# Softmax denominators of a second attention layer carried across partitions by way of DRAM in place of TensorE transposes

## The chip, the cores and the metric

The kernel runs on one core of a Trainium2 chip. The core has five engines that run side by side, each with its own queue of instructions: TensorE (PE, matrix products and transposes, with weight loads shown apart as PEld), VectorE (DVE), ScalarE (ACT), GpSimd (POOL) and SyncE (SP, which here only issues DMA transfers). SBUF and PSUM have 128 partitions. The metric is the device time of one execution in microseconds (us); lower is better. The times quoted are of whole executions, and a profile is one further execution with the hardware profiler on.

## What is computed

The reference is a trunk of two layers over 1024 positions of width 1024. The first layer is a dilated window attention in three groups; it is not touched here. The second is multi-head latent attention with 16 heads, each of 64 value columns, and it ends in a gate, an output product and a layer norm. The part that matters:

```python
def block(args):
    qn, qr = args
    s = (jnp.einsum('bqhd,bkhd->bhqk', qn, k_nope)
         + jnp.einsum('bqhd,bkd->bhqk', qr, k_rope)).astype(jnp.float32) * scale
    p = jax.nn.softmax(s, axis=-1).astype(v.dtype)
    return jnp.einsum('bhqk,bkhd->bqhd', p, v)
...
y = o * jax.nn.silu(gate)
return y @ w_out
```

The kernel does not normalise `p`. It takes exp(s - max) and its row sum, multiplies the unnormalised weights with the values, and puts the reciprocal of the row sum (the "denominator" below) into the product with the gate.

## The kernel before

The layout decides everything about the denominators. The scores of one unit `u` (head `hd = u // 8`, 128 queries `t = u % 8`) lie as queries on partitions by 1024 keys on columns, so a row sum is one number per partition. The output of weights times values (`po`) and the gate `gT` lie the other way: 64 value columns on 64 partitions, queries along the columns. So each denominator, one number on a query's partition, has to reach 64 partitions at that query's column.

The loop of `layer_b_attention` goes over 128 units, with the parts of several units interleaved:

- `front(u)`: six matmuls of 128x512 make the scores `s` (three products of split high and low parts, for two halves of the keys).
- `soft(u)`: DVE takes the row maximum, negated (L1251).
- `middle(u - 2)`: PE transposes the eight 128x128 pieces of the exponentials (L1270), ACT copies the rounded high part `pth` (L1273), DVE makes the low part `ptl` (L1274). Then DVE takes the reciprocal of the row sum (L1275), and POOL spreads it over 64 columns of a tile `den` of 128x128, one half for each unit of a pair (L1276).
- `expo(u)`: ACT takes the exponential with its row sum beside it (L1257).
- `back(w)`, once per pair of units: PE transposes `den` into columns 256 to 383 of the PSUM bank `po` (L1285), then makes 16 matmuls of weights times values into columns 0 to 255 (L1293). ACT copies the two halves of the product to SBUF (L1298, L1299). DVE multiplies the transposed denominators with the gate, in two pieces of 64x128 (L1302). POOL adds the two halves (L1305) and multiplies the sum with what DVE made, back into `gT` (L1306).

Beside the units the loop carries the preparation of the next pair of heads, step by step, in generators advanced at fixed places: `b_weights(p + 1)` loads the weights of the next pair of heads (L1109, and for every second pair L1117) and splits them into high and low parts on ACT (L1110) and POOL (L1111); `b_turn` and `b_qk` multiply with them on PE (`m` in the profile). For odd `p` the call of `b_weights(p + 1)` stands at `r = u % 16 = 1`, and the first product of `b_turn(p + 1)` follows on PE at the end of `r = 2`; for even `p` the first product with the new weights is that of `b_qk` from `r = 8` on. In the last pair of heads the loop loads the output weights (`b_wo_load`, L1353) instead. After the loop, `layer_b_out` loads rows of the norm and the gate (L781, L776) and the residual (L1395), and finishes the rows 128 at a time.

What sets the order: this part of the program stands in `tc.manual_schedule(engines=FIXED)` with `FIXED = {PE, SP}`. PE and SP run their instructions in the order in which the code writes them. The order of ACT, DVE and POOL is worked out when the program is built, from a simulated timeline. Each engine then runs its own queue strictly in order, so an instruction that waits holds all that stand behind it on its engine; SP's queue is where all loads of this layer are issued.

Two pools matter for the change: `M` (single tiles with tags) and `DR` (tiles in DRAM). `normb` and `ktab` in `layer_b_in` are two constant tables, used by `latents` (L983 to L1010) before the attention begins.

Of the kernel before, what the change touches and what calls it, by code (L numbers as in the profile page):

```python
# [15 lines left out]
F32 = mybir.dt.float32  # L16
F32R = mybir.dt.float32r
AF = mybir.ActivationFunctionType
ALU = mybir.AluOpType
# [4 lines left out]
P = 128  # L24
# [17 lines left out]
def f32(ap):  # L42
    return ap.bitcast(F32)
# [23 lines left out]
class Trunk:  # L67
# [877 lines left out]
    def layer_b_in(self):  # L945

        nc, A = self.nc, self.A
        wl = self.wl
        nb = self.M.tile([P, 384], F32, name="normb")
        nc.sync.dma_start(nb, A["bnorm"].to_broadcast([P, 384]))  # L950
        nc.vector.tensor_scalar(nb[:, 0:256], nb[:, 0:256], 96.0**-0.5, None, op0=ALU.mult)
        ktab = self.M.tile([P, 8, 2, 16], F32, name="ktab")
        nc.sync.dma_start(ktab, A["ktab"])
        U = [[(self.gt(F32R, "u1h"), self.gt(F32R, "u1l")) for _ in range(2)] for _ in range(4)]
        self.lat = [(self.gt(F32R, "lath"), self.gt(F32R, "latl")) for _ in range(3)]
# [275 lines left out]

    def layer_b_attention(self):
        nc = self.nc
        st = {}

        def front(u):
            hd, t = u // 8, u % 8
# [15 lines left out]

        def expo(u):
            s, m = st[u]
            pr = self.ht(F32, "pr")
            nc.scalar.activation(pr, s, AF.Exp, bias=m[:, 0:1], accum_out=m[:, 1:2])  # L1257
            st[u] = (pr, m)

        def middle(u):  # L1260
            pr, m = st.pop(u)
            a = u % 2
            if a == 0:
                st["pt"] = [(self.gt(F32R, "pth"), self.gt(F32R, "ptl")) for _ in range(2)]
                st["den"] = self.M.tile([P, P], F32, tag="den", bufs=3, name=self.nm("den"))
            for j in range(2):
                pt = self.PB.tile([P, 512], F32, tag="t", bufs=4, name=self.nm("t"))
                for c in range(4):
                    kt = 4 * j + c
                    nc.tensor.transpose(pt[:, c * P : c * P + P], pr[:, kt * P : kt * P + P], self.ident)  # L1270
                h, l = (x.rearrange("p (k q) -> p k q", k=4)[:, :, a * P : a * P + P] for x in st["pt"][j])
                src = pt.rearrange("p (k q) -> p k q", k=4)
                nc.scalar.copy(h, src)  # L1273
                nc.vector.tensor_tensor(l, src, f32(h), op=ALU.subtract)  # L1274
            nc.vector.reciprocal(m[:, 2:3], m[:, 1:2])  # L1275
            nc.gpsimd.tensor_copy(st["den"][:, 64 * a : 64 * a + 64], m[:, 2:3].to_broadcast([P, 64]))  # L1276
            if a:
                st[("pv", u // 2)] = (st.pop("pt"), st.pop("den"))

        def back(w):  # L1280
            pts, den = st.pop(("pv", w))
            hd, t0 = w // 4, (w % 4) * 256
            e = hd % 2
            po = self.PB.tile([P, 512], F32, tag="t", bufs=4, name=self.nm("o"))
            nc.tensor.transpose(po[:, 256:384], den, self.ident)  # L1285
            hq = hd % 4
            n = 0
            for j in range(2):
                for c in range(4):
                    kt = 4 * j + c  # L1290
                    v = self.vq[kt // 2][:, (kt % 2) * 512 + hq * P : (kt % 2) * 512 + hq * P + P]
                    for x in range(2):
                        nc.tensor.matmul(po[:, 0:256], v, pts[j][x][:, c * 256 : c * 256 + 256], start=n == 0, stop=n == 15)  # L1293
                        n += 1
            mine, other = slice(64 * e, 64 * e + 64), slice(64 - 64 * e, 128 - 64 * e)
            g = self.gT[hd // 2][mine, t0 : t0 + 256]
            w3 = self.ht(F32, "osum")
            nc.scalar.copy(w3[mine, 0:256], po[other, 0:256])  # L1298
            nc.scalar.copy(w3[mine, 512:768], po[mine, 0:256])  # L1299
            for a in range(2):  # L1300
                qs = slice(a * P, a * P + P)
                nc.vector.tensor_tensor(  # L1302
                    w3[mine, 256 + a * P : 384 + a * P], po[64 * a : 64 * a + 64, 256:384], g[:, qs], op=ALU.mult
                )
            nc.gpsimd.tensor_tensor(w3[mine, 0:256], w3[mine, 512:768], w3[mine, 0:256], op=ALU.add)  # L1305
            nc.gpsimd.tensor_tensor(g, w3[mine, 0:256], w3[mine, 256:512], op=ALU.mult)  # L1306

        nu = 128
        prep, vprep = iter(()), self.b_v(0)
# [1 line left out]
        for u in range(nu + 4):  # L1311
            p, r = u // 16, u % 16
# [22 lines left out]
            if 0 <= u - 2 < nu:  # L1335
                middle(u - 2)
                next(vprep, None)
            if u < nu:
                expo(u)
            if u == nu:  # L1340
                self.b_out_blocks(0, range(4))
            if u == nu + 1:
                self.b_out_blocks(1, range(4))
            if u >= 4 and u % 2 == 0 and u < nu + 4:
                back((u - 4) // 2)
# [194 lines left out]
```

## Time and profile before

| what | value |
|---|---|
| time of the kernel, median of 3 runs | 1395.11 us (1394.83 to 1395.6) |
| the profiled execution, whole | 1399.57 us |
| its span from first to last instruction | 1397.8 us |
| mean granted TensorE clock over the span | 0.993 |
| second attention, first to last unit (from the timeline) | about 811 to 1304 us |
| output part behind it | about 1304 to 1398 us |

The profiled execution is a little longer than the median of the timed runs, so sums made in its numbers are carried to the median as differences. In the profile a line such as `L1285 PE MATMUL o<-ident,den x64: 270/273/302` names the kernel line, the engine, the operation, the tile written and the tiles read, the count, and the least, median and largest duration in ns. Matmuls are pipelined, and the next one begins before the one before it ends, so what one costs is read from the distance between starts, which the chain of work shows. `SPq` stands for DMA issues on SP's queue. "Waits" say which engine stood still until which other one had finished.

### The profile page before, as it was taken

How to read it: one execution, taken by the hardware profiler on the slowest of the kernel's cores; microseconds unless marked ns; L12 is line 12 of the kernel's file. 1: busy time of each engine (PE TensorE's matmuls, PEld its weight loads, DVE VectorE, ACT ScalarE, POOL GpSimd, SP SyncE). 2: the span in 40 equal slices, each digit the busy share in tenths (PEclk: the TensorE clock that was granted, in tenths of full speed). 3: DMA queues.
4: the chain of work that ended last, by engine and by line, in shares of the span. 5: the costliest groups of instructions: out<-in, count | busy, mean ns of one | idle time of the engine just before them, and what ended most of it. 6: DMA issues, size and time to landing. Idle time of an engine off the chain costs nothing.

```text
span 1397.8 us, 21019 instructions
## 1 busy us (share of the span) xinstructions
PE 1355.3 (97%) x7523; PEld 1160.8 (83%) x7523; DVE 938.9 (67%) x1708; ACT 820.3 (59%) x1604; POOL 573.6 (41%) x657
## 2 busy tenths in 40 slices
PE   6999999999999999999999999999999999999897
PEld 5788888888888788888987888888889888898786
DVE  7654354555455492746745178898988889888787
ACT  3575565565443452425752178788787878888321
POOL 5341233132122226903742254634463463444653
PEclk9999999999999999999999999999999999999999
DMA  9422211022244302544145001010010100014132
GB/s 356 112 64 36 59 50 50 25 60 73 95 151 123 99 31 77 180 149 151 61 119 166 21 14 37 16 30 16 22 29 18 35 16 16 16 61 133 49 113 83
DMA packets 39721, 105.26 MB, mean 75 GB/s; under 512 B 5126, under 2 KB 11270, under 8 KB 39617
## 3 DMA queue, kind: packets, MB, share of 16 engines
q1 hardware_dynamic: 35608, 91.80, 21.3%
q0 software_dynamic: 3552, 12.06, 3.5%
q8 instruction: 60, 0.98, 0.3%
q14 instruction: 45, 0.36, 0.1%
q10 hardware_dynamic: 456, 0.05, 0.0%
HBM read 87.60 MB, written 8.43 MB: 69 GB/s over the span
## 4 chain that ended last, share of the span: by engine, by line
PE 74%; DVE 12%; ACT 5%; issue 4%; DMA 4%; SPq 0%; POOL 0%; DVEq 0%; ACTq 0%
PE pj L89 7%; PE pj L91 7%; PE pj L90 7%; PE o L1293 5%; PE t L1270 5%; PE po L89 4%; PE po L91 4%; PE po L90 4%; DVE mb L1251 3%; PE s L91 3%; PE s L89 3%; PE s L90 3%; PE pg L89 2%; PE pg L90 2%; PE pg L91 2%
## 5 line engine op out<-in xcount | busy, mean ns | idle before, releaser
L89 PE MATMUL pj<-uh,wh 128*128 128x512 f32 x528 | 216.0, 409 | 0.0
L91 PE MATMUL pj<-uh,wl 128*128 128x512 f32 x528 | 207.4, 393 | 0.0
L90 PE MATMUL pj<-ul,wh 128*128 128x512 f32 x528 | 207.4, 393 | 0.0
L1274 DVE TENSOR_TENSOR ptl<-t,pth 128x512 fp32r<-128x512 f32 x256 | 165.4, 682 | 3.0 <-ACT pth L1273 0.9
L1251 DVE TENSOR_REDUCE mb<-s 128x1 f32<-128x1024 f32 x128 | 155.8, 1217 | 7.9 <-PE s L91 6.3
L1257 ACT ACTIVATE pr<-s,mb 128x1024 f32<-128x1024 f32 x128 | 143.4, 1120 | 29.2 <-DVE mb L1251 21.1
L1273 ACT CAST pth<-t 128x512 fp32r<-128x512 f32 x256 | 138.9, 589 | 36.2 <-PE t L1270 34.1
L102 POOL TENSOR_TENSOR wl<-wraw,wh 128x1024 fp32r<-128x1024 f32 x43 | 106.6, 2485 | 106.7 <-ACT wh L101 54.6
L1270 PEld LDWEIGHTS t<-ident,pr 128*128 128x128 f32 x1024 | 119.3, 140 | 19.7 <-DVE ptl L1274 2.6
L1270 PE MATMUL t<-ident,pr 128*128 128x128 f32 x1024 | 133.2, 272 | 1.9 <-DVE ptl L1274 1.9
L1293 PE MATMUL o<-pth,vq 128*128 128x256 f32 x512 | 130.4, 292 | 0.0
L1293 PE MATMUL o<-ptl,vq 128*128 128x256 f32 x512 | 125.5, 283 | 0.8 <-DVE ptl L1274 0.8
L507 ACT ACTIVATE sb<-sb,stat 128x256 f32<-128x256 f32 (+1 forms) x144 | 67.0, 467 | 98.6 <-DVE stat L501 98.5
L91 PEld LDWEIGHTS pj<-uh,wl 128*128 128x128 f32 x528 | 99.4, 188 | 22.2
L1276 POOL COPY den<-mb 128x64 f32<-128x64 f32 x128 | 30.1, 236 | 203.2 <-DVE mb L1275 193.6
L90 PEld LDWEIGHTS pj<-ul,wh 128*128 128x128 f32 x528 | 100.1, 190 | 14.3
L89 PEld LDWEIGHTS pj<-uh,wh 128*128 128x128 f32 x528 | 99.9, 189 | 14.5
L89 PE MATMUL s<-kb,q 128*128 128x512 f32 x256 | 104.4, 408 | 0.2 <-ACT pr L1257 0.2
L91 PE MATMUL s<-kb,q 128*128 128x512 f32 x256 | 101.3, 396 | 0.0
L90 PE MATMUL s<-kb,q 128*128 128x512 f32 x256 | 100.8, 394 | 0.0
L1293 PEld LDWEIGHTS o<-ptl,vq 128*128 128x128 f32 x512 | 97.7, 191 | 1.4 <-DVE ptl L1274 1.4
L1293 PEld LDWEIGHTS o<-pth,vq 128*128 128x128 f32 x512 | 97.7, 191 | 0.2
(288 smaller groups left out, 3317.6 us busy)
## 6 DMA issues: line engine op xcount, KB each, us to landing
wraw<-wa SPq DMA_DIRECT2D x36, 512.0 KB, 4.9
ada<-ada_row SPq DMA_DIRECT2D x64, 256.0 KB, 3.6
wraw<-wo_a SPq DMA_DIRECT2D x18, 512.0 KB, 3.6
ada<-ada_ss SPq DMA_DIRECT2D x16, 512.0 KB, 8.2
kb<-kb POOLq DMA_DIRECT2D x30, 256.0 KB, 3.4
xc<-xt SPq DMA_DIRECT2D x8, 512.0 KB, 9.2
xr<-x SPq DMA_DIRECT2D x8, 512.0 KB, 5.7
xn_d<-z POOLq DMA_DIRECT2D x8, 512.0 KB, 4.6
```

Of the source, the lines that this page charges most:

```text
L89: mm(out, wh, xh, start=start, stop=False)
L90: mm(out, wh, xl, start=False, stop=False)
L91: mm(out, wl, xh, start=False, stop=stop)
L102: (lo_engine or self.nc.gpsimd).tensor_tensor(l[:, :width], raw[:, :width], f32(h[:, :width]), op=ALU.subtract)
L507: nc.scalar.activation(sb[:, a * w : a * w + w], sb[:, a * w : a * w + w], AF.Exp, bias=stat[:, 0, hh, t : t + 1], scale=-1.0, accum_out=s ...
L1251: nc.vector.tensor_reduce(m[:, 0:1], s, axis=AX.X, op=ALU.max, negate=True)
L1257: nc.scalar.activation(pr, s, AF.Exp, bias=m[:, 0:1], accum_out=m[:, 1:2])
L1270: nc.tensor.transpose(pt[:, c * P : c * P + P], pr[:, kt * P : kt * P + P], self.ident)
L1273: nc.scalar.copy(h, src)
L1274: nc.vector.tensor_tensor(l, src, f32(h), op=ALU.subtract)
L1276: nc.gpsimd.tensor_copy(st["den"][:, 64 * a : 64 * a + 64], m[:, 2:3].to_broadcast([P, 64]))
L1293: nc.tensor.matmul(po[:, 0:256], v, pts[j][x][:, c * 256 : c * 256 + 256], start=n == 0, stop=n == 15)
```

## The change

The denominators of a head are kept together in one tile `dens[hd]` of 128x8, one column per unit, written by the exponential itself. After every fourth unit, so once per 512 queries of a head (32 times in all), `spread` takes the reciprocal of four columns in one DVE instruction, stores them to a DRAM tile `den_d` so that the 512 numbers lie in the order of the queries (128 partitions with 4 numbers each, every number a separate run of 4 bytes in DRAM), and loads them back as one row of 512 numbers repeated on the 64 partitions of this head's half. Both transfers are issued on SP. The spreading on POOL (L1276), the transposes on PE (L1285) and the products on DVE (L1302) go. In `back` POOL multiplies the sum of the halves with the gate directly, and after every second pair it multiplies 64x512 of `gT` with the loaded denominators. The two tables of `layer_b_in` now use the buffers of the new tile `rden`.

```diff
--- before.py
+++ after.py
@@ -946,10 +946,11 @@
 
         nc, A = self.nc, self.A
         wl = self.wl
-        nb = self.M.tile([P, 384], F32, name="normb")
+        nb = self.M.tile([P, 512], F32, tag="rden", bufs=2, name="normb")[:, 0:384]
         nc.sync.dma_start(nb, A["bnorm"].to_broadcast([P, 384]))
         nc.vector.tensor_scalar(nb[:, 0:256], nb[:, 0:256], 96.0**-0.5, None, op0=ALU.mult)
-        ktab = self.M.tile([P, 8, 2, 16], F32, name="ktab")
+        ktab = self.M.tile([P, 512], F32, tag="rden", bufs=2, name="ktab")
+        ktab = ktab[:, 0:256].rearrange("p (i a c) -> p i a c", i=8, a=2)
         nc.sync.dma_start(ktab, A["ktab"])
         U = [[(self.gt(F32R, "u1h"), self.gt(F32R, "u1l")) for _ in range(2)] for _ in range(4)]
         self.lat = [(self.gt(F32R, "lath"), self.gt(F32R, "latl")) for _ in range(3)]
@@ -1231,7 +1232,8 @@
 
     def layer_b_attention(self):
         nc = self.nc
-        st = {}
+        st, dens, rden = {}, {}, {}
+        den_d = self.DR.tile([16, 1024], F32, name="den_d")
 
         def front(u):
             hd, t = u // 8, u % 8
@@ -1253,16 +1255,29 @@
 
         def expo(u):
             s, m = st[u]
+            hd, t = u // 8, u % 8
+            if t == 0:
+                dens[hd] = self.M.tile([P, 8], F32, tag="den", bufs=3, name=self.nm("den"))
             pr = self.ht(F32, "pr")
-            nc.scalar.activation(pr, s, AF.Exp, bias=m[:, 0:1], accum_out=m[:, 1:2])
-            st[u] = (pr, m)
+            nc.scalar.activation(pr, s, AF.Exp, bias=m[:, 0:1], accum_out=dens[hd][:, t : t + 1])
+            st[u] = pr
+
+        def spread(hd, z):
+
+
+            d = dens[hd][:, 4 * z : 4 * z + 4]
+            nc.vector.reciprocal(d, d)
+            ld = den_d[hd]
+            nc.sync.dma_start(bass.AP(ld.tensor, ld.offset + 512 * z, [[1, P], [P, 4]]), d)
+            t = rden[hd, z] = self.M.tile([P, 512], F32, tag="rden", bufs=2, name=self.nm("rden"))
+            mine = slice(64 * (hd % 2), 64 * (hd % 2) + 64)
+            nc.sync.dma_start(t[mine, :], den_d[hd : hd + 1, 512 * z : 512 * z + 512].to_broadcast([64, 512]))
 
         def middle(u):
-            pr, m = st.pop(u)
+            pr = st.pop(u)
             a = u % 2
             if a == 0:
                 st["pt"] = [(self.gt(F32R, "pth"), self.gt(F32R, "ptl")) for _ in range(2)]
-                st["den"] = self.M.tile([P, P], F32, tag="den", bufs=3, name=self.nm("den"))
             for j in range(2):
                 pt = self.PB.tile([P, 512], F32, tag="t", bufs=4, name=self.nm("t"))
                 for c in range(4):
@@ -1272,17 +1287,14 @@
                 src = pt.rearrange("p (k q) -> p k q", k=4)
                 nc.scalar.copy(h, src)
                 nc.vector.tensor_tensor(l, src, f32(h), op=ALU.subtract)
-            nc.vector.reciprocal(m[:, 2:3], m[:, 1:2])
-            nc.gpsimd.tensor_copy(st["den"][:, 64 * a : 64 * a + 64], m[:, 2:3].to_broadcast([P, 64]))
             if a:
-                st[("pv", u // 2)] = (st.pop("pt"), st.pop("den"))
+                st[("pv", u // 2)] = st.pop("pt")
 
         def back(w):
-            pts, den = st.pop(("pv", w))
+            pts = st.pop(("pv", w))
             hd, t0 = w // 4, (w % 4) * 256
             e = hd % 2
             po = self.PB.tile([P, 512], F32, tag="t", bufs=4, name=self.nm("o"))
-            nc.tensor.transpose(po[:, 256:384], den, self.ident)
             hq = hd % 4
             n = 0
             for j in range(2):
@@ -1296,14 +1308,13 @@
             g = self.gT[hd // 2][mine, t0 : t0 + 256]
             w3 = self.ht(F32, "osum")
             nc.scalar.copy(w3[mine, 0:256], po[other, 0:256])
-            nc.scalar.copy(w3[mine, 512:768], po[mine, 0:256])
-            for a in range(2):
-                qs = slice(a * P, a * P + P)
-                nc.vector.tensor_tensor(
-                    w3[mine, 256 + a * P : 384 + a * P], po[64 * a : 64 * a + 64, 256:384], g[:, qs], op=ALU.mult
-                )
-            nc.gpsimd.tensor_tensor(w3[mine, 0:256], w3[mine, 512:768], w3[mine, 0:256], op=ALU.add)
-            nc.gpsimd.tensor_tensor(g, w3[mine, 0:256], w3[mine, 256:512], op=ALU.mult)
+            nc.scalar.copy(w3[mine, 256:512], po[mine, 0:256])
+            nc.gpsimd.tensor_tensor(w3[mine, 0:256], w3[mine, 256:512], w3[mine, 0:256], op=ALU.add)
+            nc.gpsimd.tensor_tensor(g, w3[mine, 0:256], g, op=ALU.mult)
+            if w % 2:
+                z = (w % 4) // 2
+                g = self.gT[hd // 2][mine, z * 512 : z * 512 + 512]
+                nc.gpsimd.tensor_tensor(g, g, rden.pop((hd, z))[mine, :], op=ALU.mult)
 
         nu = 128
         prep, vprep = iter(()), self.b_v(0)
@@ -1337,6 +1348,8 @@
                 next(vprep, None)
             if u < nu:
                 expo(u)
+                if u % 4 == 3:
+                    spread(u // 8, (u % 8) // 4)
             if u == nu:
                 self.b_out_blocks(0, range(4))
             if u == nu + 1:
```

## The prediction

> **What bounds the kernel now.** I read the page's busy shares first, then the chain that ended last, then the stage that the change touches, cut into the 61 us that one pair of heads takes.
>
> ```profile
> PE 1355.3 (97%) x7523; PEld 1160.8 (83%) x7523; DVE 938.9 (67%) x1708; ACT 820.3 (59%) x1604; POOL 573.6 (41%) x657
> PE 74%; DVE 12%; ACT 5%; issue 4%; DMA 4%; SPq 0%; POOL 0%; DVEq 0%; ACTq 0%
> ```
>
> PE is busy for nearly the whole span and holds most of the chain. An average says little of one stage, so the next view is the table by stretches (columns: PE, PEld, DVE, ACT, POOL busy us, clock, DMA share, GB/s).
>
> ```profile
> 872.00:933.00 61.00, 59.71 (x385) 52.30 (x384) 54.96 (x96) 47.42 (x92) 33.72 (x49) 1.00 0.09 21
> 1177.00:1238.00 61.00, 60.70 (x411) 54.67 (x410) 53.54 (x94) 50.66 (x99) 21.62 (x39) 1.00 0.12 30
> sum 493.00, PE 487.36 PEld 432.49 DVE 429.67 ACT 399.91 POOL 227.90; mean PE 60.92 PEld 54.06 DVE 53.71 ACT 49.99 POOL 28.49
> ```
>
> In the second attention (the sum is over 811 to 1304 us) PE is busy 487.4 of 493 us, DVE 429.7, ACT 399.9 and POOL 227.9. PE is the bound, with DVE close behind. What PE waits for there is in the view of waits of PE (total us, times, longest):
>
> ```profile
> PE m L89 <- DVE kb L1222: 2.4, 7, 0.4
> PE t L1270 <- DVE ptl L1274: 1.9, 3, 0.6
> PE o L1293 <- DVE ptl L1274: 0.8, 3, 0.3
> PE s L89 <- ACT pr L1257: 0.2, 1, 0.2
> PE o L1285 <- DVE ptl L1274: 0.2, 1, 0.2
> ```
>
> They add up to 5.5 us, 5.3 of them on DVE. So in this stage a PE instruction taken away is worth its pitch, and work taken off DVE is worth at most these 5.3 us.
>
> **The change part by part.** First, what PE loses. The chain of waits in a stretch without preparation shows PE back to back:
>
> ```profile
> 1243.52 0.87 PE t L1270 x8
> 1244.39 0.11 PE o L1285
> 1244.50 1.91 PE o L1293 x16
> ...
> 1250.08 0.87 PE t L1270 x8
> 1250.95 0.11 PE o L1285
> 1251.06 1.91 PE o L1293 x16
> ```
>
> A pair of units takes 1250.08 - 1243.52 = 6.56 us, and the transpose of `den` is 0.11 us of it, once per pair. 64 pairs x 0.11 = **7.0 us** less on PE, all on the path.
>
> Second, what DVE and POOL lose and gain (groups by line: busy us, mean ns).
>
> ```profile
> L1302 DVE TENSOR_TENSOR osum<-o,gT 64x128 f32<-64x128 f32 x128 | 36.8, 288 | 35.5 <-ACT osum L1299 31.6 <-PE s L90 1.2 <-POOL den L1276 0.6
> L1276 POOL COPY den<-mb 128x64 f32<-128x64 f32 x128 | 30.1, 236 | 203.2 <-DVE mb L1275 193.6 <-PE t L1270 6.9 <-PE o L1293 2.4
> L1203 POOL TENSOR_TENSOR q<-rope,q 64x512 fp32r<-64x512 f32 x16 | 20.3, 1291 | 1.5 <-ACT q L1201 1.2
> L1275 DVE RECIPROCAL mb<-mb 128x1 f32<-128x1 f32 x128 | 20.0, 156 | 6.5 <-ACT pr L1257 3.7
> ```
>
> DVE loses 36.8 + 20.0 us and gains 32 reciprocals of 128x4, which I price as those of 128x1: 32 x 0.156 = 5.0. Net it loses 51.8 of 429.7 us, or 0.8 us per pair of units. The waits on `ptl` pile up over two or three pairs, in which `b_turn` adds work to DVE, to at most 0.6 us each, and those on `kb` are 0.4 us at most; 0.8 us of relief per pair should remove most of both. Between nothing and 5.5 us I take **4.0 us**. POOL loses 30.1 us and gains 32 products of 64x512. The nearest row is L1203, so 32 x 1.291 = 41.3; net 11 us more on an engine with 265 us to spare in this stage. I cost it at nothing: ACT's and DVE's work hides it, and nobody needs `gT` before the output part. ACT's two copies per pair stay as they are.
>
> Third, what the change adds to SP's queue: 64 transfers in program order among the loads. A store waits for the reciprocal, and the load behind it waits until the store has landed. Everything behind waits too. Before, SP ran far ahead:
>
> ```profile
> 860.05 0.33 SPq L1109 DMA_DIRECT2D wuraw<-wu_o  x1
> 921.28 0.33 SPq L1109 DMA_DIRECT2D wuraw<-wu_e  x1
> ```
>
> Loads are issued a whole pair of heads, some 61 us, ahead of use. After the change `b_weights(p + 1)` of unit 16p + 1 stands behind the transfers of unit 16p - 1. For even p the weights are wanted from unit 16p + 8 on, more than 20 us later; no cost. For p = 1, 3, 5 they are wanted at the end of unit 16p + 2. For p = 1 the timeline shows both ends:
>
> ```profile
> 871.47 0.19 ACT L1257 ACTIVATION_READ_ACCUMULATOR pr<-s,mb 128x1 f32 x1
> 872.73 0.15 DVE L1275 RECIPROCAL mb<-mb 128x1 f32<-128x1 f32 x1
> 880.11 0.39 PE L89 MATMUL m<-lath,wuh 128*128 128x512 f32 x1
> 880.58 0.39 PE L91 MATMUL m<-lath,wul 128*128 128x512 f32 x1
> ```
>
> The row sums of unit 15 are there at 871.66. DVE takes a reciprocal next at 872.73, behind a maximum, or earlier if it comes first, so I let the store go out at 872.4. PE wants the low part of the new weights at 880.58. Between lie the store (X), the issue of the broadcast load, the landing of the weights, and the two splits:
>
> ```profile
> DMA to landing us min/median/max: 2.4/3.3/3.9
> L1110 ACT ACTIVATE wuh<-wuraw x8: 526/636/746, 747.5 to 1163.3; 128x640 fp32r<-128x640 f32 x4, 128x384 fp32r<-128x384 f32 x4
> L1111 POOL TENSOR_TENSOR wul<-wuraw,wuh x8: 1019/1298/1579, 748.4 to 1164.4; 128x640 fp32r<-128x640 f32 x4, 128x384 fp32r<-128x384 f32 x4
> 59.99 0.29 SPq L314 DMA_DIRECT2D lines_d<-lines  x1
> 61.42 2.69 SPq L325 DMA_DIRECT2D bias<-lines_d  x6
> 15.47 0.70 SPq L289 DMA_DIRECT2D rb<-rel_bias  x1
> bias<-lines_d SPq DMA_DIRECT2D x30, 128.0 KB, 4.8
> ```
>
> Without X: 0.4 + 3.3 + 0.75 + 1.58 = 6.03 us, and 0.7 for what stands ahead of the splits on ACT and POOL (an estimate: half of one of POOL's products of 1.291 us). The slack is 880.58 - 872.4 = 8.18, so PE stands still for X - 1.45 us. X itself has no row: no transfer of the trace writes 512 runs of 4 bytes. From below, the store of `lines_d` (6 runs of 2 KB into DRAM) went out at 59.99 and its reader was issued at 61.42, so 1.4 us and no stall. From above, the loads of `bias` (128 overlapping runs of 1 KB) take 4.8 us, a stall of 3.35. The issue of a transfer of 96 runs of 24 bytes took 0.70 us instead of 0.3, so many small runs cost issue time. Nearest in kind is the store of `lines_d`; with 0.4 more for issue and 0.6 for the number of runs X = 2.4, a stall of 1.0 us, three times: **+3.0 us** (0 to 10).
>
> The Trainium skill speaks against this transfer. "DMA: Bandwidth & Descriptors", section "Rules for kernel authors", says that a strided last dimension makes one descriptor per element, and its section "Specifications" that pieces under 512 B are written by read-modify-write. Its section "Anatomy of one DMA" has a fixed cost of about 2.0 us per transfer, which would make X 2.0 and the stall 0.55; the store above, at 1.4, is under that figure.
>
> The load of the denominators itself is not on this path. Taking the 4.5 us of the similar broadcast `row<-rows_d`, it lands at about 872.4 + 2.4 + 4.5 = 879.3, and POOL wants it behind the gate product:
>
> ```profile
> row<-rows_d SPq DMA_DIRECT2D x2, 512.0 KB, 4.5
> 882.31 0.74 POOL L1306 TENSOR_TENSOR gT<-osum 64x256 f32<-64x256 f32 x1
> ```
>
> That leaves 3 us of slack; past it POOL would hold `osum` and rope work, of which it has time to make up.
>
> Fourth, the tail. The last denominators leave with unit 127 (reciprocal at 1291.13), and the rows of the norm are issued behind them:
>
> ```profile
> 1283.86 4.30 SPq L781 DMA_DIRECT2D lnrow<-ln  x4
> 1291.13 0.15 DVE L1275 RECIPROCAL mb<-mb 128x1 f32<-128x1 f32 x1
> 1308.70 1.99 ACT L1390 ACTIVATE lnrow<-lnrow 128x1024 f32<-128x1024 f32 x2
> 1317.80:1320.90 3.10, 0.18 (x1) 0.00 (x0) 3.07 (x3) 0.63 (x1) 3.10 (x2) 0.91 0.00 0
> 1320.90:1327.00 6.10, 6.03 (x14) 4.77 (x15) 5.40 (x5) 1.26 (x2) 6.10 (x3) 0.50 0.00 0
> ```
>
> They would go out at about 1294 and be there by 1299; ACT uses them at 1308.70. So nothing is late. The two other rows show that PE stands still for about 3 us at 1318 while DVE works, and that the granted clock is 0.50 for some 6 us behind it. That hole costs about 3 + 3 us. POOL's one more product (1.3 us) and DVE's two fewer (0.6 us) could shift it either way, by -6 to +2.6; I take 0.
>
> Sum: -7.0 - 4.0 + 3.0 + 0 = **-8.0 us**. The profiled execution of 1399.57 (span 1397.8) would be 1391.6; carried to the median, 1395.11 - 8.0 = **1387.1 us**.
>
> **The rivals.**
>
> - *Slower: the store is slow.* If X is 4.45 us or more, the stall at p = 1, 3, 5 reaches 3 us, the length that in the tail was followed by about 6 us at half clock. Then each costs X - 1.45 + 3, and from there the three outweigh the 11 us. At X = 4.8: 3 x (3.35 + 3) = 19, minus 11, so +8 us: 1403. For it: 512 runs, no row like it, and a queue strictly in order. Against it: the only store into DRAM whose end shows took 1.4 us, and SP's issue of small runs only 0.70. By the Trainium skill's "TensorE: Matmul & The Clock Gate", section "HAM oscillation — how this bites in real kernels", idle gaps over about 3.4 us halve the clock; the trace has it behind about 3 us. By that rule a stall of 3.35 us would stay under it, and X = 4.8 would give 3 x 3.35 - 11 = -1 us, an estimate.
> - *No difference: ACT waits for the weights.* The split L1110 sits in ACT's fixed order. If that order takes the load to be quicker than it is, the exponentials behind it wait, at all six preparations from p = 1 on, at perhaps 1 us each, beside the 3 us: -11 + 3 + 6 = -2 us: 1393. For it: ACT is busy 400 of 493 us; against: the load's 2.4 to 3.9 us vary little.
> - *More than forecast.* All waits on DVE go, X hides, and the hole in the tail closes: -7.0 - 5.5 - 6 = -18.5: 1376.6. For it: DVE has relief everywhere; against: DVE's own chain in the tail is hardly touched.
>
> **How the numbers follow.** What a measurement can tell from no change is about 0.2%, or 2.8 us. Forecast (between -3 and -13 us): 0.60. More: 0.10. No difference: 0.15. Slower: 0.15. So faster 0.70, same 0.15, slower 0.15. The forecast's own range, with X from 1.4 to 3.5 and DVE's waits from 2 to 5.5, is 1382 to 1391. Half of the chance of "more" reaches below 1380, and the slow store's milder half (X just past 4.45) gives about 1400; I give 1380 to 1399.
>
> **What would show it.** Right: pairs of units 6.45 us apart where they were 6.56; no rows for L1275's 128x1, L1276, L1285, L1302; DVE near 378 us in the stage; PE's waits on `kb` and `ptl` mostly gone. The stores' landing shows in SP's wait between store and load. A PE wait before `m` of L89 at the third unit of odd pairs gives X. Wrong: a clock under 1.00 inside the attention, ACT waiting at L1110 for `wuraw`, POOL waiting for `rden`, or a longer hole at 1318.

## The result, and the profile after

The changed kernel takes **1459.51 us** (median of 4 runs, 1457.13 to 1460.66), the kernel before on the same chip 1395.36 (1394.83 to 1395.79). The ratio is 1.0461 (95% interval 1.0448 to 1.0474): 64 us slower, where 8 us faster was forecast and 1399 was the end of the range. The profiled execution took 1460.36 us, its span is 1458.6 us, its mean granted clock 0.973 (before 0.993).

The page of the changed kernel first: busy shares, the granted clock in 40 slices, and the chain that ended last.

```profile
PE 1364.9 (94%) x7459; PEld 1167.4 (80%) x7459; DVE 890.0 (61%) x1484; ACT 817.7 (56%) x1604; POOL 585.5 (40%) x561
PEclk9999999999999999999999998999899899999998
PE 63%; DMA 11%; DVE 11%; ACT 9%; issue 5%; POOL 1%; SPq 1%; DVEq 0%; ACTq 0%; POOLq 0%
```

PE has its 64 transposes less (7459 for 7523) and DVE is 49 us less busy, so the work that should go has gone. But PE's share of the chain fell from 74% to 63% and DMA's rose from 4% to 11%, and the clock has dips, where that row showed a 9 in all 40 slices before. The table by stretches (PE, PEld, DVE, ACT, POOL busy us, clock, DMA share, GB/s) shows how much of one pair of heads is lost:

```profile
872.00:933.00 61.00, 48.27 (x275) 41.20 (x274) 37.28 (x51) 35.64 (x69) 29.81 (x30) 0.86 0.11 23
1177.00:1238.00 61.00, 55.50 (x354) 48.92 (x353) 42.47 (x59) 46.20 (x90) 28.78 (x33) 0.97 0.17 30
```

In the first 61 us PE does 275 matmuls where it did 385. The view of waits over the second attention (engine and line waited for, total us, times, longest) names what stands still. L1111 is the split of the weights that was L1110 before, L1317 POOL's new product.

```profile
POOL gT L1317 <- DMA rden<-den_d: 52.9, 15, 13.0
ACT wuh L1111 <- DMA wuraw<-wu_e: 25.8, 3, 9.1
ACT wuh L1111 <- DMA wuraw<-wu_o: 23.5, 3, 8.5
PE m L89 <- ACT wuh L1111: 20.9, 3, 7.4
ACT wh L101 <- DMA woraw<-wo_b: 18.7, 3, 7.9
PE m L89 <- DVE ptl L1289: 15.3, 3, 5.7
PE t L1285 <- ACT osum L1311: 14.1, 3, 5.5
```

ACT waits nine times for a load of weights: at all six preparations of a pair of heads and three times for output weights in the last pair. PE's three rows are the echo: 20.9 + 15.3 + 14.1 = 50.3 us, in nine waits too. Three stand directly behind the split; in the six others the name (`ptl`, `osum`) is only the last link, for ACT's queue is in order and what PE waits for stood behind the split. The chain of waits through one of the nine shows the links, and the two windows behind it the clock:

```profile
1012.51 0.18 DVE den L1269
...
1012.71 8.09 DMA den_d<-den
...
1020.85 0.45 SPq L1274
...
1021.35 4.43 DMA wuraw<-wu_e
...
1025.80 0.74 ACT wuh L1111
...
1026.67 1.55 POOL wul L1112
...
1028.27 0.80 PE m L91
1029.07 0.43 PE m L89
```

```profile
1020.60:1027.20 6.60, 0.61 (x2) 0.50 (x2) 0.00 (x0) 1.40 (x3) 0.53 (x1) 0.65 0.41 89
1028.00:1036.00 8.00, 7.73 (x29) 6.21 (x29) 6.24 (x10) 3.91 (x9) 6.21 (x7) 0.70 0.00 1
```

The reciprocal is done at 1012.69. The store's landing takes 8.09 us more, only then may SP issue the load of the denominators, and the weights' load stands behind that. PE works 0.61 us in 6.60, and then its matmuls run 0.43 us apart, where 0.23 is the pitch at full clock. The landing of the stores, by the view of their line (the trace ties a landing to its issue for 5 of the 32), and SP's two waits:

```profile
DMA to landing us min/median/max: 8.7/8.9/13.2
```

```profile
SPq L1274 <- DMA den_d<-den: 277.3, 31, 12.6
SPq L1271 <- DVE den L1269: 268.8, 29, 55.1
```

SP's wait for the stores is 277.3 us in 31 waits, 8.9 us each, so the five stand for the rest. X was put at 2.4 us, with 4.8 as the upper end.

One measure is used below for every kernel: the **stage**, from the start of the first matmul of scores to the start of the last matmul of weights times values, as the timeline of its profiled execution has them. Before it is 1304.91 - 813.85 = 491.1 us, after 1367.30 - 810.58 = 556.7. What follows the stage takes 92.9 us before and 91.3 after. So the loss, 65.7 us in these executions, is all inside the second attention. (The whole spans differ by 60.8 us, since the stage also begins 3.3 us earlier after the change.)

The distances between the starts of PE's matmuls divide it. Distances over 1.5 us beyond the median of their kind: nine after, together 51.9 us, and none in the stage before. Smaller excesses in the stage (0.06 to 1.5 us each) went from 21.2 to 39.2 us, and 23.3 of the 39.2 lie within 10 us behind one of the nine, where the granted clock is 0.50 to 0.72 over the next 6 us. That is 51.9 + 18.0 = 69.9 us; less the 7.0 of the transposes that are gone it makes 62.9 of the 65.7.

### The profile page after: what moved, and what is told of

Read it like the earlier page. It is cut to its first block, busy times and chain, and to the rows that moved or that the text cites. A ratio compares the mean times of both kernels' runs of the same rounds, so it can differ in the third digit from the quotient of the medians.

```text
span 1458.6 us, 20417 instructions
## 1 busy us (share of the span) xinstructions
PE 1364.9 (94%) x7459; PEld 1167.4 (80%) x7459; DVE 890.0 (61%) x1484; ACT 817.7 (56%) x1604; POOL 585.5 (40%) x561
## 4 chain that ended last, share of the span: by engine, by line
PE 63%; DMA 11%; DVE 11%; ACT 9%; issue 5%; POOL 1%; SPq 1%; DVEq 0%; ACTq 0%; POOLq 0%
PE pj L89 7%; PE pj L90 7%; PE pj L91 7%; DMA den_d<-den 6%; PE o L1305 4%; PE t L1285 4%; PE po L91 3%; PE po L89 3%; PE po L90 3%; PE s L89 2%; PE s L90 2%; PE s L91 2%; PE pg L89 2%; PE pg L90 2%; PE pg L91 2%
## 5 line engine op out<-in xcount | busy, mean ns | idle before, releaser
L1253 DVE TENSOR_REDUCE mb<-s 128x1 f32<-128x1024 f32 x128 | 155.9, 1218 | 51.9 <-PE s L91 50.7
L1285 PE MATMUL t<-ident,pr 128*128 128x128 f32 x1024 | 137.8, 279 | 14.1 <-ACT osum L1311 14.1
L1285 PEld LDWEIGHTS t<-ident,pr 128*128 128x128 f32 x1024 | 123.2, 144 | 32.3 <-ACT osum L1311 14.9
L1312 POOL TENSOR_TENSOR osum<-osum 64x256 f32<-64x256 f32 x64 | 47.5, 742 | 160.6 <-ACT osum L1311 156.0
L90 PEld LDWEIGHTS pj<-ul,wh 128*128 128x128 f32 x528 | 99.9, 189 | 14.1
L89 PE MATMUL s<-kb,q 128*128 128x512 f32 x256 | 107.3, 419 | 0.0
L90 PE MATMUL s<-kb,q 128*128 128x512 f32 x256 | 103.3, 403 | 0.0
L91 PE MATMUL s<-kb,q 128*128 128x512 f32 x256 | 102.7, 401 | 0.0
```

The source lines that it names most:

```text
L89: mm(out, wh, xh, start=start, stop=False)
L90: mm(out, wh, xl, start=False, stop=False)
L91: mm(out, wl, xh, start=False, stop=stop)
L1253: nc.vector.tensor_reduce(m[:, 0:1], s, axis=AX.X, op=ALU.max, negate=True)
L1312: nc.gpsimd.tensor_tensor(w3[mine, 0:256], w3[mine, 256:512], w3[mine, 0:256], op=ALU.add)
```

## The experiments

Times are medians, and each ratio is to the kernel before on the same chip (1394.2 to 1395.7). "Landing" is the median, in us from issue, of those of the 32 stores whose landing the trace tells: all in c_poolq and l_pool16, 13 or 14 in d_later, i_spaced, g_runs8, a_runs16, h_both and k_early16, 5 in the changed kernel, 4 in e_early9 and j_plus, none in b_otherdata.

| kernel | what differs from the changed kernel | time, us | ratio, interval | stage, us | landing, us |
|---|---|---|---|---|---|
| changed | | 1459.51 | 1.0461 [1.0448, 1.0474] | 556.7 | 8.9 |
| f_none | no transfers | 1385.93 | 0.9936 [0.9921, 0.9952] | 482.7 | |
| b_otherdata | load independent of the store | 1443.55 | 1.0347 [1.0330, 1.0363] | 539.3 | |
| d_later | load three units later | 1460.46 | 1.0463 [1.0442, 1.0483] | 559.7 | 8.7 |
| i_spaced | b_otherdata, runs 64 bytes apart | 1386.54 | 0.9951 [0.9934, 0.9967] | 483.7 | 1.9 |
| c_poolq | b_otherdata, store on POOL's queue | 1388.88 | 0.9968 [0.9958, 0.9979] | 485.2 | 8.5 |
| g_runs8 | 256 runs of 8 bytes | 1402.48 | 1.0063 [1.0043, 1.0083] | 498.5 | 3.1 |
| a_runs16 | 128 runs of 16 bytes | 1394.08 | 0.9991 [0.9981, 1.0000] | 490.1 | 1.4 |
| e_early9 | weights loaded 8 units earlier | 1429.22 | 1.0253 [1.0234, 1.0272] | 524.9 | 8.2 |
| h_both | a_runs16, weights 4 units earlier | 1400.75 | 1.0044 [1.0023, 1.0065] | 495.7 | 1.5 |
| k_early16 | a_runs16, weights 8 units earlier | 1389.74 | 0.9963 [0.9950, 0.9977] | 484.6 | 1.4 |
| l_pool16 | a_runs16, both transfers on POOL's queue | 1389.75 | 0.9970 [0.9959, 0.9982] | 486.6 | 1.7 |
| j_plus | the kernel before, plus the transfers | 1466.18 | 1.0511 [1.0495, 1.0527] | 562.1 | 8.0 |

The theory at the start: SP's wait for a slow store delays everything queued behind it. The rival: the small writes hold the other transfers themselves, whether SP waits or not.

### f_none: the parts taken out, alone

The two transfers go; POOL multiplies with a constant tile instead, so the denominators are left out.

```diff
+        rone = self.M.tile([P, 512], F32, tag="rden", bufs=2, name="rone")
+        nc.sync.dma_start(rone, self.A["ln"][0:1, 0:512].to_broadcast([P, 512]))
...
-            nc.sync.dma_start(bass.AP(ld.tensor, ld.offset + 512 * z, [[1, P], [P, 4]]), d)
...
-            nc.sync.dma_start(t[mine, :], den_d[hd : hd + 1, 512 * z : 512 * z + 512].to_broadcast([64, 512]))
...
-                nc.gpsimd.tensor_tensor(g, g, rden.pop((hd, z))[mine, :], op=ALU.mult)
+                nc.gpsimd.tensor_tensor(g, g, rone[mine, :], op=ALU.mult)
```

> The changed kernel without the 64 transfers: the reciprocals are taken but go nowhere, and the product uses one row of ln loaded once, so the division by the denominators is left out. It prices the first two steps of the forecast by themselves. By the forecast -7.0 us on PE and -4.0 us of waits on DVE: 1384 us, between 1382 and 1388. Rival O (the new order of ACT, DVE and POOL or POOL's wider product costs by itself): 1393 us or more.

1385.93 us, 9 us under the kernel before (its interval is 6.7 to 11 us); the stage is 8.4 us shorter. What is taken out is worth a little less than the 11 us of the forecast; the transfers cost 1459.5 - 1385.9 = 73.6 us. How the gain is made up is seen in the chain without preparation and in the waits of PE:

```profile
1239.28 1.91 PE o L1301 x16
...
1245.73 1.91 PE o L1301 x16
```

```profile
PE m L89 <- DVE kb L1223: 3.7, 7, 0.5
PE t L1281 <- DVE ptl L1285: 1.9, 3, 0.6
```

A pair of units takes 6.45 us, 0.11 less than before, as forecast. But PE's waits on DVE are still there: 5.6 us, for 5.3 before. DVE has 46 us less to do (893.1 us busy over the span, for 938.9) and PE waits for it as long.

### a_runs16: the same numbers in 128 runs of 16 bytes

Each partition's four numbers stay together in DRAM, and POOL reads the loaded row with a step of 4.

```diff
-            nc.sync.dma_start(bass.AP(ld.tensor, ld.offset + 512 * z, [[1, P], [P, 4]]), d)
+            nc.sync.dma_start(bass.AP(ld.tensor, ld.offset + 512 * z, [[4, P], [1, 4]]), d)
...
-                nc.gpsimd.tensor_tensor(g, g, rden.pop((hd, z))[mine, :], op=ALU.mult)
+                g = g.rearrange("p (c q) -> p c q", c=4)
+                r = rden.pop((hd, z))[mine, :].rearrange("p (q c) -> p c q", c=4)
+                nc.gpsimd.tensor_tensor(g, g, r, op=ALU.mult)
```

> The changed kernel with the store laid out as 128 runs of 16 bytes (each partition's four numbers side by side) and the product on POOL reading the loaded row with a step of 4. Theory S (the 512 runs of 4 bytes make the store land after 8.9 us, and SP's queue is held that long): the landing falls to 2 to 3 us and the time to 1384 to 1393 us. Rival R (a store to DRAM that is read back costs about 9 us however it is cut): landing 8 to 9 us and 1450 to 1460 us. A landing between, 4 to 6 us, would give some 1395 to 1425 us, since only stalls over about 3 us halve the clock.

```profile
DMA to landing us min/median/max: 1.4/1.4/2.7
```

```profile
ACT wuh L1111 <- DMA wuraw<-wu_o: 5.2, 3, 2.6
ACT wuh L1111 <- DMA wuraw<-wu_e: 3.4, 3, 1.4
```

The landing falls from 8.9 to 1.4 us and the time to 1394.08, even with the kernel before. The same 2 KB, the same queue and the same waits cost 65 us less with another layout in DRAM. (POOL's product, the other difference, makes POOL busier: 594.4 us for 585.5.) ACT's waits at `wuh` shrink from 49.3 to 8.6 us and do not go: the weights' loads still stand behind a store and a load.

### b_otherdata and d_later: is it SP's wait?

In b_otherdata the load reads a row of another tensor, so it needs no store, and SP never waits for one (the denominators are left out of the result). In d_later the load is issued three units after its store and the product comes one pair later, so that the weights' loads pass SP ahead of the wait.

```diff
# b_otherdata
-            nc.sync.dma_start(t[mine, :], den_d[hd : hd + 1, 512 * z : 512 * z + 512].to_broadcast([64, 512]))
+            nc.sync.dma_start(t[mine, :], self.A["ln"][0:1, 512 * z : 512 * z + 512].to_broadcast([64, 512]))
```

```diff
# d_later
+        def fetch(n):
+            hd, z = n // 2, n % 2
...
+            if w % 2 == 0 and w:
+                scale(w // 2 - 1)
...
+            if u % 4 == 2 and u >= 6:
+                fetch((u - 6) // 4)
```

> The changed kernel with its slow store kept, but the load reads an input row (a row of ln) in place of the denominators, so SP waits for no landing; the division by the denominators is thereby replaced by a product with other numbers. Theory S (the wait on the landing, not the traffic, is the cost): 1384 to 1392 us, ACT's waits on the weights gone. Rival T (512 small writes per transfer slow the other transfers or engines): 1430 us or more with the wait gone.

> The changed kernel with the load issued three units after its store, and the product with the denominators one pair later; the store is as slow as before. Theory S with what stands behind the wait as the victim (the weights' loads now pass ahead of the wait): 1384 to 1395 us with landings still 8 to 9 us. Rival P (POOL waiting for the denominators, 52.9 us in the profile, is what holds the rest): POOL's waits must vanish too for a gain; if the weights alone mattered, POOL may still wait and the time be the same. If the store's landing slows PE in some other way: above 1430 us.

Both kernels stay slow: 1443.55 and 1460.46. The theory that SP's wait is the main cost fell here. SP's timeline and ACT's in b_otherdata, and SP's in d_later, with d_later's waits:

```profile
867.05 0.37 SPq L1271 DMA_DIRECT2D den_d<-den  x1
867.52 0.47 SPq L1274 DMA_DIRECT2D rden<-ln  x1
868.04 0.58 SPq L1110 DMA_DIRECT2D wuraw<-wu_e  x1
```

```profile
879.08 0.74 ACT L1111 ACTIVATE wuh<-wuraw 128x640 fp32r<-128x640 f32 x1 [7.74 <-DMA wuraw<-wu_e]
```

```profile
866.52 0.36 SPq L1271 DMA_DIRECT2D den_d<-den  x1
866.93 0.97 SPq L1110 DMA_DIRECT2D wuraw<-wu_e  x1
```

```profile
ACT wuh L1111 <- DMA wuraw<-wu_e: 29.8, 3, 10.5
ACT wuh L1111 <- DMA wuraw<-wu_o: 25.1, 3, 9.0
```

In b_otherdata the weights' load goes out 1 us behind the store, as early as SP can, and is there 11 us later. In d_later it is issued 0.4 us behind the store, with no wait between, and ACT waits longer for these loads than in the changed kernel; PE has nine stops there too. Without a store beside it this load took 2.4 to 3.9 us in the kernel before. So a load that is issued while such a store is in flight comes late with it. SP's wait, which the changed kernel has on top, is worth 1459.5 - 1443.6 = 16 us, together with POOL's wait for `rden`.

### i_spaced and g_runs8: the number of runs, or their neighbourhood?

i_spaced is b_otherdata with the 512 runs of 4 bytes placed 64 bytes apart (denominators left out likewise). g_runs8 writes pairs: 256 runs of 8 bytes, with the full computation.

```diff
# i_spaced
-        den_d = self.DR.tile([16, 1024], F32, name="den_d")
+        den_d = self.DR.tile([32, 8192], F32, name="den_d")
...
-            ld = den_d[hd]
+            ld = den_d[2 * hd + z]
-            nc.sync.dma_start(bass.AP(ld.tensor, ld.offset + 512 * z, [[1, P], [P, 4]]), d)
+            nc.sync.dma_start(bass.AP(ld.tensor, ld.offset, [[16, P], [16 * P, 4]]), d)
```

```diff
# g_runs8
-            nc.sync.dma_start(bass.AP(ld.tensor, ld.offset + 512 * z, [[1, P], [P, 4]]), d)
+            nc.sync.dma_start(bass.AP(ld.tensor, ld.offset + 512 * z, [[2, P], [256, 2], [1, 2]]), d.rearrange("p (a b) -> p a b", a=2))
... (POOL's product reads the loaded row in the matching order)
```

> The stores keep their 512 runs of 4 bytes, but each run lies 64 bytes from the next one in DRAM; as in b_otherdata the loads read a row of ln, so the denominators are left out of the result. Theory N, the number of runs sets the landing: about 8.9 us as in b_otherdata, time 1440 to 1447. Theory A, what costs is that neighbouring runs share a block of DRAM: landing 1.5 to 3 us, time 1384 to 1392.

> The same 512 numbers stored as 256 runs of 8 bytes in place of 512 of 4; the reader undoes the order. Landings so far: 8.9 us for 512 runs, 1.4 us for 128. Theory N, landing grows with the number of runs: 1.4 + 7.5 x 128/384 = 3.9 us, so the held-up shrinks by 5 us at each place and falls to 1 to 3 us, mostly under what halves the clock: 1396 to 1412. Rival, any run under 16 bytes is slow in itself: landing 6 us or more and 1425 to 1455.

The landing rows of the stores, i_spaced first, then g_runs8:

```profile
DMA to landing us min/median/max: 1.7/1.9/2.9
```

```profile
DMA to landing us min/median/max: 2.7/3.1/4.0
```

i_spaced is the clearest pair of the study: the same number of runs, of the same size, on the same queue, with the same loads behind them, and 1386.54 us in place of 1443.55. 57 us go with the distance between the runs in DRAM alone. So neither the count of runs nor their 4 bytes makes the store slow by itself, but that such pieces lie side by side. Why that is slow no run here shows, nor what distance below 64 bytes would do. g_runs8 by itself met theory N's time and came near its landing (3.1 us for 3.9), and its rival, that every run under 16 bytes is slow, fell; but its runs are half as many and have half as many neighbours, so it can't tell number from neighbourhood, and i_spaced, which can, refutes N.

By the Trainium skill, "DMA: Bandwidth & Descriptors", section "Specifications", pieces under 512 B are written by read-modify-write. All stores here have pieces far under it, and their landings run from 1.4 to 8.9 us, so that rule alone gives no price.

### c_poolq: does another queue help?

b_otherdata with the store issued on POOL's queue; the loads stay on SP.

```diff
-            nc.sync.dma_start(bass.AP(ld.tensor, ld.offset + 512 * z, [[1, P], [P, 4]]), d)
+            nc.gpsimd.dma_start(bass.AP(ld.tensor, ld.offset + 512 * z, [[1, P], [P, 4]]), d)
```

> The stores of 512 single numbers are kept, but they go out on POOL's queue, and as in b_otherdata the loads on SP read a row of ln, so SP waits for no store (the denominators are left out of the result). Theory Q, the held-up is in SP's own queue (a load stands behind the store only where both are on the same queue): wuraw lands 3 to 4 us after its issue again and the time is that of f_none, 1384 to 1392. Theory E, the small writes hold the transfer engines as such, whichever queue they come from: wuraw still lands 8 us or more after an issue that falls beside a store, PE stands still at the same six places, 1430 to 1450.

By time, 1388.88, this looks like theory Q: the loads were held only by their own queue. The landings say otherwise. The rows of the stores, of `rden`'s loads and of `woraw`'s (landings known for 32, 11 and 3 of them), in this order, and `woraw`'s in the kernel before:

```profile
DMA to landing us min/median/max: 8.0/8.5/11.3
```

```profile
DMA to landing us min/median/max: 2.7/3.5/7.6
```

```profile
DMA to landing us min/median/max: 7.5/8.5/8.8
```

```profile
DMA to landing us min/median/max: 3.3/3.3/3.6
```

The output weights' loads on SP take 8.5 us beside stores on POOL's queue, where they took 3.3 in the kernel before and 3.9 in i_spaced (one known landing). A load of `rden` issued 0.09 us behind a store (986.99 behind 986.90) landed after 7.6 us; one issued at 876.73, with no store in flight, after 2.8. So the held-up crosses queues, as theory E has it. The time is good for another reason, which neither theory had seen: SP no longer holds the stores, so it waits for no reciprocal and runs ahead, and loads that come late are still early enough. The `wuraw` load that b_otherdata issued at 868.04 goes out here at 849.44, and ACT's waits at `wuh` are 4.5 us in all, for 44.8 in b_otherdata. This fits the Trainium skill, "DMA: Bandwidth & Descriptors", section "Queues, rings and completion order": a transfer's completion lands only after every earlier write of the same DMA engine, across its queues. No run here tells that rule from writes that simply keep the memory busy.

### e_early9, h_both, k_early16: the weights out of the way

All three split `b_weights` in two and issue its loads earlier, between two stores: after unit 16p + 9 (e_early9, with the slow store of the change; k_early16, with runs of 16 bytes), or after unit 16p + 13 (h_both, runs of 16 bytes).

```diff
+    def b_weights_load(self, p):
+        nc, A, BS = self.nc, self.A, self.BS
+        raw = BS.tile([P, 640], F32, tag="wuraw", bufs=1, name=self.nm("wuraw"))
+        n = 384 if p % 2 else 640
+        nc.sync.dma_start(raw[:, 0:n], A["wu_o" if p % 2 else "wu_e"][p // 2])
...
+                if r == 9 and p + 2 < NPAIR_B:
+                    self.b_weights_load(p + 2)
```

> The changed kernel with its slow stores, but the weights of the next pair of heads are loaded eight units earlier (after unit 16p + 9, between two stores, when none is in flight). My theory (the loss is mainly that the weights' loads stand behind or beside a store in flight): ACT's 49 us of waiting for wuraw go with PE's six stops and the half clock behind them; what stays is the last pair of heads, where the output weights are still loaded between stores (18.7 us of ACT's waits), so 1400 to 1418. Rival, POOL's 53 us of waiting for rden, which hold osum and through it PE, are as much of it: 1425 to 1450.

> Stores of 128 runs of 16 bytes as in a_runs16, and the weights of the next pair of heads are loaded three units before the store that they stood behind. My theory (what is left of a_runs16 over f_none, 1394.1 to 1385.9, is ACT's waits of 3.4 to 5.2 us for wuraw behind transfers): ACT no longer waits at wuh, 1386 to 1389, faster than both kernels. Rival, the left 8 us are POOL's product with strided reads or the transfers' own traffic: 1391 to 1395, ACT's waits gone and nothing won.

> h_both with the weights loaded after unit 16p + 9 in place of 16p + 13. In h_both ACT still waited up to 4.1 us for wuraw, since ACT's order put the split ahead of where the load landed. My theory: with four units (15 us) more the load has landed, no wait of ACT at wuh is left and the time is that of f_none plus at most 3 us: 1385 to 1389. Rival, the transfers themselves or POOL's strided product cost the rest: 1392 to 1396.

e_early9 came out at 1429.22, in the rival's range and not by the rival's mechanism: PE's stops fell from nine to five. SP's timeline and ACT's at the first of them:

```profile
835.73 0.38 SPq L1284 DMA_DIRECT2D den_d<-den  x1
843.64 0.46 SPq L1287 DMA_DIRECT2D rden<-den_d  x1
844.20 0.53 SPq L1107 DMA_DIRECT2D wuraw<-wu_e  x1
844.77 0.42 SPq L1111 DMA_DIRECT2D wvraw<-wv  x1
```

```profile
848.80 0.42 ACT L1132 ACTIVATE wvh<-wvraw 128x256 fp32r<-128x256 f32 x1 [7.01 <-DMA wvraw<-wv]
```

The loads are no longer beside a store, and land 4 us after their issue. But they are issued only once SP's wait for the store before is over, at 844.20, and ACT has stood at the split of the value weights (L1132) since 841.79, before that load was even issued. ACT's order is worked out when the program is built, and the split moves in it with the load: by ACT's timelines this first split of value weights stands behind the 18th exponential in the changed kernel, behind the 13th in h_both and behind the 9th here. So moving a load ahead moved the wait to another place. (That the plan takes the load to land sooner than it does is a reading that fits.)

h_both shows the same with the fast store. It is slower (1400.75) than a_runs16 without the move (1394.08): both theories missed. ACT's timeline:

```profile
860.38 0.74 ACT L1125 ACTIVATE wuh<-wuraw 128x640 fp32r<-128x640 f32 x1 [4.06 <-DMA wuraw<-wu_e]
```

The load had gone out at 857.08 by SP's timeline, and ACT waits 4.06 us for it. k_early16, four units earlier still, does what h_both was meant to: no wait of ACT for `wuraw` is left (1.2 us for `wvraw` are), and the time is **1389.74 us**, ratio 0.9963 (0.9950 to 0.9977), just above the 1385 to 1389 of my theory. With l_pool16 it is the fastest version that computes everything, and it beats both kernels: 4.7 us (0.4%) under the kernel before, 70 under the changed one.

### l_pool16: both transfers off SP

```diff
# against a_runs16
-            nc.sync.dma_start(bass.AP(ld.tensor, ld.offset + 512 * z, [[4, P], [1, 4]]), d)
+            nc.gpsimd.dma_start(bass.AP(ld.tensor, ld.offset + 512 * z, [[4, P], [1, 4]]), d)
...
-            nc.sync.dma_start(t[mine, :], den_d[hd : hd + 1, 512 * z : 512 * z + 512].to_broadcast([64, 512]))
+            nc.gpsimd.dma_start(t[mine, :], den_d[hd : hd + 1, 512 * z : 512 * z + 512].to_broadcast([64, 512]))
```

> Stores of 128 runs of 16 bytes as in a_runs16, but stores and loads of the denominators both go out on POOL's queue, so SP runs ahead with the weights as before the change. My theory: ACT does not wait for wuraw; POOL pays 64 issues of about 0.8 us (51 us) and stands about 1.5 us at each store, and has some 230 us to spare in the stage: 1386 to 1392. Rival, POOL waiting for its own store holds the additions of osum and the low parts of the weights, and PE stops for them: 1394 to 1410.

1389.75 us, as my theory had it: SP runs ahead again, the weights land in 3.3 us, ACT does not wait for `wuraw`. POOL waits 11.8 us for its own stores and has the time.

### j_plus: the kernel before with the transfers added

Nothing is taken out; the added store and load run beside the old way, and nobody reads what they bring.

```diff
# against before
+        def spread(hd, z, m):
+            d = self.M.tile([P, 4], F32, tag="dsum", bufs=3, name=self.nm("dsum"))
+            nc.vector.reciprocal(d, m[:, 1:2].to_broadcast([P, 4]))
...
+                if u % 4 == 3:
+                    spread(u // 8, (u % 8) // 4, st[u][1])
```

> The kernel before, with nothing taken out, and beside it the added transfers alone: after every fourth unit one reciprocal of four columns (of the one row sum at hand, so not the denominators), the store of 512 runs of 4 bytes and the load that waits for it, whose result nobody reads. If the transfers are the whole of the loss (after against f_none: 1459.5 - 1385.9 = 73.6 us), the time is 1395 + 60 to 75 = 1455 to 1470; if the loss needs POOL's product waiting for rden, 1415 to 1450; if it comes from the parts taken out, 1395 to 1400.

```profile
ACT wuh L1110 <- DMA wuraw<-wu_o: 26.5, 3, 8.9
ACT wuh L1110 <- DMA wuraw<-wu_e: 24.7, 3, 8.4
```

1466.18 us, 71.8 us over the kernel before (1394.41), against the 73.6 from the other side. ACT's waits are those of the changed kernel (25.8 and 23.5 there). So the transfers alone are the loss, and POOL's product waiting for `rden` isn't needed for it. That speaks for SP's wait, and not POOL's, behind the 16 us between the changed kernel and b_otherdata.

## Why the prediction was wrong

By its own steps:

1. **PE's transposes, -7.0: right.** Pairs of units are 6.45 us apart, as said.
2. **Relief of DVE, -4.0: wrong, and small.** f_none's stage is 8.4 us shorter, which leaves 1.4 for this term, and not by the way foreseen. PE's waits on `kb` and `ptl` did not shrink (5.6 for 5.3 us), so they do not come from DVE's load as a whole. The step took a lower total for a shorter wait at one place; that a wait ends with a chain of PE, ACT and DVE, and not with DVE's queue, is only argued, and what the 1.4 us are stays open. POOL's new product took 1.284 us, by the row chosen 1.291.
3. **SP's queue, +3.0: this step failed, and it decides.** It rests on X, the store's landing, put at 2.4 us between bounds of 1.4 and 4.8. It was 8.9. The rows that I took for neighbours (a store of 6 runs of 2 KB, a load of runs of 1 KB) have nothing to do with what made it slow: i_spaced shows that 512 runs of 4 bytes land in 1.9 us when they lie apart, and a_runs16 that 128 runs of 16 bytes take 1.4. The text said that X had no row, and then let two far rows bound it from above. The figure of 2.0 us that it took beside them from the Trainium skill, "DMA: Bandwidth & Descriptors", section "Anatomy of one DMA", is given there for transfers issued from GpSimd, and these stores go out on SP.
   A second assumption failed with it: that transfers share nothing but SP's order. b_otherdata and d_later have no wait of SP between the store and the weights' load, and the load is late all the same: b_otherdata still costs 1443.55 - 1385.93 = 57.6 us of the 73.6, d_later all of it. A stall of X - 1.45 could not have given that.
   The third: only three places were priced. For even p the weights were to have 20 us in hand, and the last pair's output weights weren't priced at all. ACT waited in all nine places: its fixed order has the six splits behind the 18th, 34th, 50th, 66th, 82nd and 98th exponential, so at the same place for even p as for odd, however late PE needs them. This was the rival "ACT waits for the weights", at 1 us each; the nine waits were 6.2 to 8.6 us each in the mean of their three rows.
4. **The tail, 0: right, in part by luck.** What follows the stage took 91.3 us after, 92.9 before. But the hole at 1318 did close: PE waits 0.6 us for `zb` where it waited 3.0, and the granted clock behind it is 1.00 where it was 0.50. From the end of the stage to PE's last matmul the tail became 5.3 us shorter, and what follows the start of that matmul 3.7 us longer (12.0 for 8.3). Why the end became longer is open.

Of the rivals, "the store is slow" had most of the mechanism (X over 4.45, stops over 3 us, a lower clock behind each; not that the load itself comes late) and put it at 1403, as it went no higher than X = 4.8 and three places. With X = 8.9 its own formula gives 3 x (8.9 - 1.45 + 3) = 31 us at three places and 94 at nine, where the transfers cost 73.6. Of the four signs named for a wrong forecast three are there: a clock under 1.00 in the attention, ACT at the split, POOL at `rden`; the hole at 1318 did not grow. The forecast's own range was added up a little short as well: with X at 3.5 and 2 us of DVE's waits it is -7.0 - 2.0 + 3 x 2.05 = -2.9, which makes 1392 and not 1391. The range ended at 1399 all the same, too near for a duration that no row of the trace showed.

## What to carry to other kernels

A DMA of small pieces is priced by how the pieces lie in DRAM, and by what is in flight beside it; where the trace shows no transfer of that pattern, leave its time open by several times, and write the layout so that one partition's numbers stay together, or lie apart (64 bytes here, measured for the store alone, with a reader that did not need it). Before adding a transfer to a queue that feeds an engine with an order fixed at build time, list every load that can be in flight with it, not only those whose use is near: late loads stop that engine where the plan expected them. Moving a load ahead helps only if its issue really comes earlier on the chip; look at the issue in SP's timeline against the place of its reader in the fixed order.

## What was not expected of the hardware

- 512 neighbouring pieces of 4 bytes, 2 KB in all, land after 8.9 us; 64 bytes apart after 1.9; as 256 pieces of 8 bytes after 3.1, as 128 of 16 after 1.4.
- While such a store is in flight, loads land late on other queues as well: 8.5 for 3.3 us (`woraw` in c_poolq).
- The granted clock falls behind holes shorter than the 3 us that the prediction took from the tail, and not always. In f_none a hole of 1.94 us at 1304.85 is followed by 0.72 over 6 us (second row); k_early16, with one of 2.20 us at the same place, keeps 1.00:

```profile
1304.50:1307.00 2.50, 0.74 (x4) 0.28 (x2) 2.50 (x3) 0.63 (x1) 2.50 (x2) 1.00 0.00 0
1307.00:1313.00 6.00, 5.98 (x19) 4.78 (x20) 5.30 (x4) 1.26 (x2) 6.00 (x3) 0.72 0.00 1
```

```profile
1306.90:1309.60 2.70, 0.66 (x4) 0.24 (x3) 2.70 (x3) 0.63 (x1) 2.70 (x2) 1.00 0.00 0
1309.60:1315.00 5.40, 5.40 (x25) 4.41 (x25) 4.70 (x4) 1.27 (x2) 5.40 (x3) 1.00 0.00 0
```

  By the Trainium skill, "TensorE: Matmul & The Clock Gate", section "HAM oscillation — how this bites in real kernels", it takes gaps over about 3.4 us; the first of these two kernels does not agree.
